# A packed 16-bit copy of the weights' high parts for the down projection's second matmul

## The chip, the cores and the metric

One core of one Trainium2 chip runs the whole kernel as one launch. The metric is the device time of that launch in microseconds; lower is better. A kernel is timed in several runs and its median is compared. Of each kernel one further execution is recorded by the hardware profiler; the profile's durations are from that one.

## What is computed

The reference is one layer of a hybrid decoder block on 512 tokens of width 2048, all in float32. The change lies in the last matrix product, the down projection of the gated feed-forward part:

```python
def conv_ffn(h, w_up, conv_w, conv_b, w_down):
    u = h @ w_up                                   # (512, 2048) @ (2048, 11264)
    ...                                            # three-tap convolution along the tokens
    val, gate = jnp.split(c, 2, axis=-1)
    return (jax.nn.silu(gate) * val) @ w_down      # (512, 5632) @ (5632, 2048)

def reference(x, ...):
    ...                                            # RWKV-7 mixing and windowed attention, gated
    x = x + (g_rw * p_rw + g_att * p_att) @ w_out[l]
    x = x + conv_ffn(rms_norm(x, norm2_g[l]), w_up[l], conv_w[l], conv_b[l], w_down[l])
    return x
```

## The kernel before

**Three matmuls for one product.** Every float32 product is made of three matmuls that add up in one PSUM tile. Each operand is split into a high part (ScalarE's copy to `float32r`, TensorE's reduced float32 format) and a low part (VectorE's difference of the operand and its high part, in bfloat16). The three are high x high, low x high and high x low. For the latter two the high part is taken as bfloat16, and there is no copy for that: `top(x)` views the float32r tile as 16-bit elements and takes every second one, the upper half of each word. So a tile of 1024 words is read as 1024 16-bit elements at a step of 4 bytes.

```python
    def top(x):
        x = x.bitcast(BF16)
        return x[(slice(None),) * (len(x.shape) - 1) + (slice(1, None, 2),)]
```

**The stages.** The program runs in this order: projections of the normed input (`project`, L284), among which attention and the recurrent mixing are woven; branch projections (L284 too, in `project`); the output projection; the up projection with the convolution; the down projection. In `project` the weights are the stationary operand and the activations the moving one. Its third matmul moves `top(xhi)`, or, once it exists, `x16`, a packed bfloat16 copy that lies in the second half of the tile `xlo` (the profile names it xlo). In the branch projections the activations are named `rhi, rlo, ahi, alo` and have no such copy.

**Output and down projection** are each cut into two by two blocks and made of seven block products in place of eight (`PRODUCTS`), on sums and differences of blocks. Each product accumulates in a set of four PSUM tiles, `X` or `Y` by turns, and is then added into the result (`taken_out`; for the down projection into `xa`, L1102, which the outputs are stored from). The sums of weight blocks were made long before by accumulating DMAs (`sums_along`, issued by SP and POOL) into DRAM. For the down projection the order of the work is: product i of seven, step c of 11 (`NB["dn"]`), half q of two.

**One step** is `steps_of` (L1070 on). The activations' part (`fetch`, L1064 on) is a 128 x 2 x 256 tile `hraw`, loaded by SP and split into `hhi` (ScalarE, L216) and `hlo` (VectorE, L217). For each q, SP loads a 128 x 1024 weight tile (L1078, six buffers), ScalarE makes `whi` (L1080), VectorE makes `wlo` (L1081), with three buffers of each. Here the roles are turned: the activations are stationary and the weights are the moving operand, 512 columns at a time. Twelve matmuls follow (L1090): three kinds by two row blocks by two column blocks. In the code's words the kinds are (stationary, moving) = (`hhi`, `whi`), (`hlo`, `top(whi)`), (`top(hhi)`, `wlo`); the profile writes a matmul's two inputs as moving,stationary: `whi,hhi` (float32), `whi,hlo` and `wlo,hhi` (16-bit). The order of the kinds alternates, `turns = ((0, 1, 2), (1, 2, 0))`: for q = 0 first whi,hhi, then whi,hlo, then wlo,hhi; for q = 1 first whi,hlo, then wlo,hhi, then whi,hhi. So whi,hhi matmuls of two tiles stand together.

**What sets the order around it.** Each engine takes its instructions in program order; waits between engines come from the tile framework, by who last wrote or read a buffer. So ScalarE's next `whi` waits for the last reader of the buffer three tiles back, and TensorE's matmuls wait for the splits. POOL (GpSimd) computes nothing in the output, up or down projection but two small memsets: it issues accumulating DMAs during the earlier stages, and at step 1 of the down projection's first product the four loads of `xa` (L1508). At that same point the pools of tiles of the up projection (`upcx`, `upx`) are closed and their memory becomes free.

Of the kernel before, what the change touches and what calls it, by code (L numbers as in the profile page):

```python
# [11 lines left out]
BF16 = mybir.dt.bfloat16  # L12
# [7 lines left out]
P = 128  # L20
# [115 lines left out]
def block_kernel(ctx: ExitStack, tc: tile.TileContext, d: Dims, a: dict, out: bass.AP):  # L136
    nc = tc.nc
    act, dve, pool, pe, sync = nc.scalar, nc.vector, nc.gpsimd, nc.tensor, nc.sync
# [54 lines left out]
    def rsqrt_small(pl, ss, scale, eps, mx=None, tag="rq"):  # L193
        n = ss.shape[-1]
        tl = [pl.tile([P, 8], F32, name=f"{tag}{i}", tag=f"{tag}{i}", bufs=2)[:, :n] for i in range(3)]
        v, y, t = tl
        if mx is not None:
            dve.tensor_scalar(v, ss, mx, None, op0=ALU.max)
        else:
            dve.tensor_scalar(v, ss, scale, eps, op0=ALU.mult, op1=ALU.add)  # L200
        dve.tensor_scalar(t.bitcast(I32), v.bitcast(I32), 1, None, op0=ALU.logical_shift_right)
        dve.tensor_scalar(y.bitcast(I32), t.bitcast(I32), -1, 0x5F3759DF, op0=ALU.mult, op1=ALU.add)
        dve.tensor_scalar(v, v, -0.5, None, op0=ALU.mult)
        for _ in range(3):
            dve.tensor_tensor(t, y, y, op=ALU.mult)
            dve.tensor_tensor(t, t, v, op=ALU.mult)
            dve.scalar_tensor_tensor(y, t, 1.5, y, op0=ALU.add, op1=ALU.mult)
        return y
# [11 lines left out]
    def quarter(w, src, c):  # L220
        return sum_d[w][src][c] if isinstance(src, str) else a["w_" + w][src[0], src[1], 2 * c : 2 * c + 2]

    jobs, up_jobs = [], []
    for f in range(NPRE):
        w, t = a["w_up"][f], {n: up_d[f, n] for n in ("s3", "s1", "P6", "P3")}
# [22 lines left out]
# [3 lines that stand above are left out]
# [45 lines left out]
    if True:  # L296
# [39 lines left out]
        def ztile(c0):  # L336
            acc = accp.tile([P, S], F32, name="acc", tag="acc")
            project(acc, zt[c0], xhi, xlo, x16 if scaled else None, first.pop(c0, ()))
            return acc
# [5 lines left out]
        r = rsqrt_small(p0, ssum, 1.0 / d.D, RMS_EPS)  # L345
# [58 lines left out]
        with ExitStack() as pt:  # L404
# [59 lines left out]
            for t in range(1, NKV):  # L464
                for c0, then in ((d.c_ka, keys), (d.c_va, values)):
                    acc = ztile(c0 + t * P)
# [25 lines left out]
            for g in range(NHK):  # L492
# [7 lines left out]
                for n in range(NT):  # L500
                    ts = slice(n * P, (n + 1) * P)
# [15 lines left out]
                    mx, es, den, rc = (st[:, i] for i in range(4))  # L517
# [34 lines left out]
        with ExitStack() as pr:  # L552
# [30 lines left out]
            acc = ztile(d.c_wd)  # L583
# [5 lines left out]
            acc = ztile(d.c_ad)  # L589
# [3 lines left out]
            for i in range(NG):  # L593
                acc = ztile(d.c_gd + i * P)
# [403 lines left out]
    hp0 = hps.enter_context(tc.tile_pool(name="hhlC", bufs=2, side="right", reuse_waits="tile"))  # L998
    wp["step"] = 12
    with ExitStack() as pbb:  # L1000
# [8 lines left out]
        for m, i in order:  # L1009
# [10 lines left out]
            acc = accp.tile([P, S], F32, name="acc", tag="acc")  # L1020
            project(acc, a["w_b"][m].rearrange("p (k c) -> p k c", c=P)[:, r0 : r0 + n], hi, lo)
            if second:
                w = min(XC, d.D)
# [31 lines left out]
    WC = KH * P  # L1055

    def raw_tile(nm="raw", n=6):
        return rwp.tile([P, WC], F32, name=nm, tag=nm, bufs=n)

    def banks(pl, nm):  # L1060
        return [[pl.tile([P, S], F32, name=f"{nm}{t}{q}") for q in range(NQW)] for t in range(NT // 2)]

    def fetch(w, i, c, pl, pin=free):

        hhi, hlo = (pl.tile([P, 2, TH], t, name=f"h{e}", tag=f"h{e}") for e, t in (("hi", F32R), ("lo", BF16)))
        hr = pl.tile([P, 2, TH], F32, name="hraw", tag="hraw")
        pin(sync.dma_start(hr, right_d[w][c][RIGHT_AT[PRODUCTS[i][3]]]))
        return lambda: split(hhi, hlo, hr, pin), hhi, hlo

    def steps_of(w, i, acc, c, pl, got=None):  # L1070

        _, start, src, _, _ = PRODUCTS[i]
        make, hhi, hlo = got or fetch(w, i, c, pl)
        if not got:
            make()
        for q in range(2):
            wr = raw_tile()
            sync.dma_start(wr, quarter(w, src, c)[q])  # L1078
            whi, wlo = (hlp.tile([P, WC], t, name=f"w{e}", tag=f"w{e}") for e, t in (("hi", F32R), ("lo", BF16)))
            act.activation(whi, wr, AF.Copy)  # L1080
            dve.tensor_tensor(wlo, wr, whi.bitcast(F32), op=ALU.subtract)  # L1081
            fst, lst = start and c + q == 0, c == NB[w] - 1 and q == 1
            order = turns[q]
            for j in order:
                for t in range(NT // 2):
                    ts = slice(t * P, (t + 1) * P)
                    for e in range(NQW):
                        dst, es = acc[t][e], slice(e * S, (e + 1) * S)
                        l, r = ((hhi[:, q, ts], whi[:, es]), (hlo[:, q, ts], top(whi[:, es])), (top(hhi[:, q, ts]), wlo[:, es]))[j]
                        pe.matmul(dst, l, r, start=fst and j == order[0], stop=lst and j == order[2],  # L1090
                                  skip_group_check=True)

    def taken_out(i, acc, xr, scale, done):
        ci, tj, sign = PRODUCTS[i][4]
        last = i in (3, 4, 5, 6)
        for t in range(NT // 2):
            for e in range(NQW):
                tt = tj * NT // 2 + t
                cs = slice(ci * DH + e * S, ci * DH + (e + 1) * S)
                x = xr(tt, cs)  # L1100
                if scale == 1.0:
                    dve.tensor_tensor(x, x, acc[t][e], op=ALU.add if sign > 0 else ALU.subtract)  # L1102
                else:
                    (pin if i == 6 else free)(
                        dve.scalar_tensor_tensor(x, acc[t][e], sign * scale, x, op0=ALU.mult, op1=ALU.add))
                if last:
                    done(i, tt, ci * NQW + e, cs)
# [264 lines left out]
    with tc.tile_pool(name="sqp", bufs=1, side="right", reuse_waits="tile") as sqp:  # L1372
        yx = ExitStack()
        py = yx.enter_context(tc.tile_pool(name="psY", bufs=1, space=PSUM, side="right", reuse_waits="tile"))
        acc = {"X": banks(px, "X"), "Y": banks(py, "Y")}
        for i in range(len(PRODUCTS)):
            nm = PRODUCTS[i][0]
# [98 lines left out]
    hp0 = upcx.enter_context(tc.tile_pool(name="hhl0", bufs=1, side="right", reuse_waits="tile"))  # L1476
# [3 lines left out]
    for i in range(4 * NPRE + 3, len(steps)):  # L1480
        run(i)
        if steps[i] == (NF - 2, "P7"):
            first_h = fetch("dn", 0, 0, hp0, pin)
# [8 lines left out]
    with ExitStack() as pd:  # L1492
        pxy = pd.enter_context(tc.tile_pool(name="psD", bufs=1, space=PSUM, reuse_waits="tile"))
        acc = {n: banks(pxy, n) for n in "YX"}
        for i in range(len(PRODUCTS)):
            nm = PRODUCTS[i][0]
            for c in range(NB["dn"]):
                if i == 0 and c == 1:
                    while later:
                        later.pop(0)()  # L1500
                    B[-1].keep()
                    upcx.close()
                    upx.close()
                    hp0 = pd.enter_context(tc.tile_pool(name="hhl", bufs=3, reuse_waits="tile"))
                    xp = pd.enter_context(tc.tile_pool(name="xacc", bufs=1, reuse_waits="tile"))
                    xa = xp.tile([P, NT, d.D], F32, name="xa")
                    for t in range(NT):
                        pool.dma_start(xa[:, t], x1_d[t * P : (t + 1) * P])  # L1508
                steps_of("dn", i, acc[nm], c, hp0, first_h if i == 0 and c == 0 else None)
            taken_out(i, acc[nm], lambda t, cs: xa[:, t, cs], 1.0, row_out)  # L1510


# [57 lines left out]
def build(nc, arrays, d):  # L1570
    aps = {
        k: nc.dram_tensor(f"in_{k}_dram", v.shape, mybir.dt.from_np(v.dtype), kind="ExternalInput").ap()
        for k, v in arrays.items()
    }
    out = nc.dram_tensor("out_0_dram", (S, d.D), F32, kind="ExternalOutput").ap()
    with tile.TileContext(nc) as tc:
        block_kernel(tc, d, aps, out)
# [11 lines left out]
```

## Time and profile before

| what | value |
| --- | --- |
| median of 3 runs | 2712.91 us (2708.49 to 2714.39) |
| the profiled execution | 2711.84 us, of which 2710.1 us span |
| TensorE matmul busy | 2670.9 us, 99% of the span |
| VectorE busy | 1961.6 us, 72% |
| ScalarE busy | 1332.1 us, 49% |
| POOL busy | 233.4 us, 9% |
| TensorE clock granted, mean | 0.997 |

PE is TensorE's matmuls, PEld its weight loads, DVE is VectorE, ACT ScalarE, POOL GpSimd, SP the engine that only issues DMAs. A row of a group reads: line, engine, operation, output<-inputs by tile name, shapes, x count, then busy us, mean ns of one, and after the bar the idle time of that engine just before such instructions and what ended it. A row of the chain or the timeline begins with the start and the length in us from the start of the span. Successive matmuls overlap in the records and their ends are modelled, so the mean of one is longer than its share of the time; the spacing of starts is the better measure of the rate.

### The profile page before, as it was taken

The page shows a single profiled execution, that of the slowest core. Times are in us where ns is not written, and L with a number is a line of the kernel's source. Part 1 is how long each engine was busy: PE and PEld are TensorE (multiplying, and loading weights), DVE is VectorE, ACT ScalarE, POOL GpSimd, SP SyncE. Part 2 cuts the span into 40 slices and gives each one's busy share as a digit, 9 for nine tenths or more (in the row PEclk, how much of TensorE's full clock was granted, in tenths as well). Part 3 has the DMA queues.
Part 4 walks back from the last instruction along what each step waited for, and adds up shares of the span by engine and source line. Part 5 has one row for each costly group of instructions (what it writes and reads, how often), then busy time and mean ns, then how long its engine had stood idle before and what let it go on. Part 6 is the DMA issues. An engine that isn't in the chain of part 4 may idle for free.

```text
span 2710.1 us, 45707 instructions
## 1 busy us (share of the span) xinstructions
PE 2670.9 (99%) x17410; PEld 1863.9 (69%) x17410; DVE 1961.6 (72%) x3380; ACT 1332.1 (49%) x2229; POOL 233.4 (9%) x322
## 2 busy tenths in 40 slices
PE   8999999999999999999999999999999999999999
PEld 4555566666666666555558898999999998555555
DVE  6787768776877774555678788888878888665655
ACT  6455445544544453322566555555554555444453
POOL 0001011111111101011000011111111110000000
PEclk9999999999999999999999999999999999999999
DMA  6566887889887778888776888988899888877775
GB/s 236 150 165 180 216 219 197 223 221 232 218 222 194 197 181 253 245 249 283 249 256 190 238 227 243 251 245 238 242 247 252 236 238 280 303 240 249 256 260 182
DMA packets 228331, 623.78 MB, mean 230 GB/s; under 512 B 24960, under 2 KB 45072, under 8 KB 227088
## 3 DMA queue, kind: packets, MB, share of 16 engines
q1 hardware_dynamic: 159552, 445.23, 49.8%
q0 software_dynamic: 37216, 136.33, 26.3%
q10 hardware_dynamic: 31344, 39.31, 4.2%
q8 instruction: 136, 2.23, 0.3%
q14 instruction: 83, 0.68, 0.1%
HBM read 571.16 MB, written 191.18 MB: 281 GB/s over the span
## 4 chain that ended last, share of the span: by engine, by line
PE 82%; DVE 8%; DMA 3%; issue 3%; ACT 2%; POOL 0%; SPq 0%; ACTq 0%; DVEq 0%; POOLq 0%
PE acc L284 26%; PE X L1227 16%; PE X L1090 11%; PE Y L1090 9%; PE Y L1227 8%; PE Z L1227 4%; DVE wlo L264 1%; PE psG L836 1%; PE psS L852 1%; PE bulk L711 1%; DMA raw<-in_w_z_dram 1%; PE bulk L760 1%; PE mi L541 1%; DVE wlo L1209 1%; PE psU L841 1%
## 5 line engine op out<-in xcount | busy, mean ns | idle before, releaser
L1081 DVE TENSOR_TENSOR wlo<-raw,whi 128x1024 bf16<-128x1024 f32 x210 | 256.7, 1225 | 192.7 <-ACT whi L1080 191.7
L284 PE MATMUL acc<-xhi,whi 128*128 128x512 f32 x1152 | 348.9, 427 | 10.9 <-ACT whi L263 10.4
L1080 ACT ACTIVATE whi<-raw 128x1024 fp32r<-128x1024 f32 x210 | 221.9, 1058 | 276.0 <-PE X L1090 119.5
L263 ACT ACTIVATE whi<-raw 128x512 fp32r<-128x512 f32 x352 | 218.8, 627 | 254.3 <-PE acc L284 151.4
L264 DVE TENSOR_TENSOR wlo<-raw,whi 128x512 bf16<-128x512 f32 x352 | 239.9, 688 | 136.8 <-ACT whi L263 113.9
L284 PE MATMUL acc<-xlo,whi 128*128 128x512 bf16 x1152 | 315.3, 382 | 0.5 <-ACT whi L263 0.3
L284 PE MATMUL acc<-xlo,wlo 128*128 128x512 bf16 x1072 | 292.9, 380 | 0.0
L1209 DVE TENSOR_TENSOR wlo<-raw,whi 128x1024 bf16<-128x1024 f32 x184 | 224.8, 1223 | 72.9 <-ACT whi L1207 72.1
L1227 PEld LDWEIGHTS <-wlo 128*128 128x128 bf16 x2464 | 237.1, 97 | 42.1 <-DVE wlo L1209 2.6
L284 PEld LDWEIGHTS acc<-xhi,whi 128*128 128x128 f32 x1152 | 212.6, 190 | 59.5 <-ACT whi L263 11.9
L1227 PEld LDWEIGHTS <-whi 128*128 128x128 bf16 x2464 | 228.3, 98 | 36.3 <-ACT whi L1207 2.3
L1207 ACT ACTIVATE whi<-a 128x1024 fp32r<-128x1024 f32 x124 | 130.7, 1054 | 229.8 <-DVE a L1202 210.9
L284 PEld LDWEIGHTS <-wlo 128*128 128x128 bf16 x1408 | 137.4, 99 | 149.6 <-issue 7.9
L284 PEld LDWEIGHTS <-whi 128*128 128x128 bf16 x1408 | 125.6, 100 | 151.0 <-issue 48.6
L1209 DVE TENSOR_TENSOR wlo<-a,whi 128x1024 bf16<-128x1024 f32 x124 | 151.9, 1225 | 64.0 <-ACT whi L1207 62.8
L1227 PE MATMUL X<-b,whi 128*128 128x256 f32 (+1 forms) x1472 | 195.7, 281 | 0.4 <-DVE u L1249 0.2
L1207 ACT ACTIVATE whi<-raw 128x1024 fp32r<-128x1024 f32 x184 | 192.1, 1046 | 5.7 <-PE Y L1227 2.6
L1227 PE MATMUL X<-t,whi 128*128 128x256 bf16 (+1 forms) x1408 | 186.2, 281 | 2.9 <-ACT u L1255 2.9
L1227 PE MATMUL Y<-t,whi 128*128 128x256 f32 (+1 forms) x1408 | 186.4, 280 | 0.3 <-DVE u L1257 0.3
L1090 PEld LDWEIGHTS <-hhi 128*128 128x128 bf16 x840 | 81.5, 97 | 103.9
L1090 PEld LDWEIGHTS <-hlo 128*128 128x128 bf16 x840 | 72.8, 97 | 107.4 <-issue 27.4
L1279 DVE SCALAR_TENSOR_TENSOR c<-u,par,c 128x512 f32<-128x512 f32 x176 | 131.4, 747 | 14.2 <-ACT c L1276 14.1
(390 smaller groups left out, 4593.9 us busy)
## 6 DMA issues: line engine op xcount, KB each, us to landing
raw<-in_w_up_dram SPq DMA_DIRECT2D x170, 512.0 KB
raw<-in_w_z_dram SPq DMA_DIRECT2D x288, 256.0 KB
s_dn<-in_w_dn_dram POOLq DMA_DIRECT2D x88, 512.0 KB, 7.2
raw<-s_dn SPq DMA_DIRECT2D x88, 512.0 KB
raw<-in_w_up_dram POOLq DMA_DIRECT2D x80, 512.0 KB, 8.2
raw<-in_w_dn_dram SPq DMA_DIRECT2D x66, 512.0 KB
s_dn<-in_w_dn_dram SPq DMA_DIRECT2D x44, 512.0 KB
s_dn<-s_dn SPq DMA_DIRECT2D x44, 512.0 KB
```

What stands on the lines that cost most here:

```text
L263: act.activation(hi, raw, AF.Copy)
L264: dve.tensor_tensor(lo, raw, hi.bitcast(F32), op=ALU.subtract)
L284: stream.append(pe.matmul(acc, l, r, start=k0 + j == 0, stop=k0 + n == nk and j == len(ops) - 1))
L541: pe.matmul(ps, vhl[:, n - 1 + kb, g].rearrange("p e c -> p (e c)"), phl[i][:, kb].rearrange("p h c -> p (h c)"), start=kb == kbs[0] and i ...
L711: pe.matmul(ps[:, j * 2 * P : (j + 1) * 2 * P], BKK[:, n0 + j], BAR[:, n0 + j].rearrange("p h a c -> p (h a c)"), start=True, stop=True)
L1080: act.activation(whi, wr, AF.Copy)
L1081: dve.tensor_tensor(wlo, wr, whi.bitcast(F32), op=ALU.subtract)
L1090: pe.matmul(dst, l, r, start=fst and j == order[0], stop=lst and j == order[2], skip_group_check=True)
L1207: pin(act.activation(hi, t, AF.Copy))
L1209: return lambda: pin(dve.tensor_tensor(lo, t, hi.bitcast(F32), op=ALU.subtract))
L1227: pin(pe.matmul(ps, l, r, start=start and k == 0 and i == way[0], stop=k == KH - 1 and i == way[2], skip_group_check=True))
L1279: pin(dve.scalar_tensor_tensor(t, u[:, i, j + 1 : j + 1 + S], cw[:, j + 1, ci : ci + 1], t, op0=ALU.mult, op1=ALU.add))
```

## The change

From the second of the seven products of the down projection on, a new pool `flat` with three buffers holds `w16`, a packed bfloat16 tile of 128 x 1024. For each weight tile POOL copies `top(whi)` into it, and the second kind of matmul moves `w16` in place of `top(whi)`. The numbers are the same, since the copy keeps the 16 bits. The first product of the down projection, and the whole output projection, which `steps_of` serves too, stay as they were, because `flat` is `None` there. The stationary operand `top(hhi)` of the third kind stays strided.

```diff
-    def steps_of(w, i, acc, c, pl, got=None):
+    def steps_of(w, i, acc, c, pl, got=None, flat=None):
...
             dve.tensor_tensor(wlo, wr, whi.bitcast(F32), op=ALU.subtract)
+            w16 = top(whi)
+            if flat:
+                w16 = flat.tile([P, WC], BF16, name="w16", tag="w16")
+                pool.tensor_copy(w16, top(whi))
             fst, lst = start and c + q == 0, c == NB[w] - 1 and q == 1
...
-                        l, r = ((hhi[:, q, ts], whi[:, es]), (hlo[:, q, ts], top(whi[:, es])), (top(hhi[:, q, ts]), wlo[:, es]))[j]
+                        l, r = ((hhi[:, q, ts], whi[:, es]), (hlo[:, q, ts], w16[:, es]), (top(hhi[:, q, ts]), wlo[:, es]))[j]
...
         acc = {n: banks(pxy, n) for n in "YX"}
+        flat = None
         for i in range(len(PRODUCTS)):
             nm = PRODUCTS[i][0]
+            if i == 1:
+                flat = pd.enter_context(tc.tile_pool(name="w16", bufs=3, reuse_waits="tile"))
...
-                steps_of("dn", i, acc[nm], c, hp0, first_h if i == 0 and c == 0 else None)
+                steps_of("dn", i, acc[nm], c, hp0, first_h if i == 0 and c == 0 else None, flat)
```

## The prediction, made before the changed kernel was run

> **What bounds the kernel now.** I read the page's shares first, then the chain of waits in order of time.
>
> ```profile
> PE 2670.9 (99%) x17410; PEld 1863.9 (69%) x17410; DVE 1961.6 (72%) x3380; ACT 1332.1 (49%) x2229; POOL 233.4 (9%) x322
> PE 82%; DVE 8%; DMA 3%; issue 3%; ACT 2%; POOL 0%; SPq 0%; ACTq 0%; DVEq 0%; POOLq 0%
> ```
>
> ```profile
> 2289.01 59.35 PE X L1090 x264
> 2348.36 59.33 PE Y L1090 x264
> ...
> 2585.67 59.33 PE Y L1090 x264
> 2644.99 58.64 PE X L1090 x261
> ```
>
> The second fence is the end of the chain: start, length, what. From 2289 us on the chain is nothing but the down projection's matmuls: seven block products of 264 matmuls, 59.33 us each, with nothing between. So here time is what TensorE's matmuls take, and only two things can change it: a shorter matmul, or a wait that opens a gap. Next, the same stretch by windows (PE, PEld, DVE, ACT, POOL busy, then the clock, DMA share, GB/s).
>
> ```profile
> 2289.01:2348.36 59.35, 59.35 (x265) 32.74 (x265) 40.36 (x47) 30.14 (x36) 2.15 (x4) 1.00 0.90 340
> 2348.36:2407.69 59.33, 59.33 (x265) 32.75 (x265) 35.97 (x39) 28.99 (x33) 0.00 (x0) 1.00 0.74 244
> 2585.67:2644.99 59.32, 59.32 (x265) 32.74 (x265) 35.91 (x39) 28.99 (x33) 0.00 (x0) 1.00 0.76 260
> ```
>
> PE has no gap and a granted clock of 1.00; DVE is busy 35.97 of 59.33 us; POOL does nothing from the second product on, which is where the change gives it work. Now the groups by line in five of those products (2348.36 to 2644.99 us), and the same view of an earlier stage, the branch projections (1060 to 1235 us); columns are busy us, then mean ns.
>
> ```profile
> L1081 DVE TENSOR_TENSOR wlo<-raw,whi 128x1024 bf16<-128x1024 f32 x110 | 134.8, 1225 | 114.2 <-ACT whi L1080 113.7
> L1080 ACT ACTIVATE whi<-raw 128x1024 fp32r<-128x1024 f32 x110 | 116.4, 1059 | 151.7 <-PE Y L1090 83.5 <-PE X L1090 55.7 <-DVE xa L1102 12.5
> L1090 PE MATMUL Y<-whi,hhi 128*128 128x512 f32 x264 | 73.0, 416 | 0.0
> L1090 PE MATMUL Y<-whi,hlo 128*128 128x512 bf16 x264 | 70.7, 389 | 0.0
> L1090 PE MATMUL Y<-wlo,hhi 128*128 128x512 bf16 x264 | 67.6, 378 | 0.0
> L217 DVE TENSOR_TENSOR hlo<-hraw,hhi 128x512 bf16<-128x512 f32 x55 | 37.6, 684 | 0.0
> L1102 DVE TENSOR_TENSOR xa<-xa,X 128x512 f32<-128x512 f32 x12 | 7.4, 682 | 1.6 <-PE X L1090 1.6
> ```
>
> ```profile
> L284 PE MATMUL acc<-ahi,wlo 128*128 128x512 bf16 x108 | 28.8, 387 | 0.0
> L284 PE MATMUL acc<-alo,whi 128*128 128x512 bf16 x109 | 28.2, 380 | 0.0
> L284 PE MATMUL acc<-xlo,wlo 128*128 128x512 bf16 x56 | 14.4, 379 | 0.0
> ```
>
> Both 16-bit products of L1090 stream 512 columns, yet the one with hlo takes 389 ns and the one with hhi 378. In the first the moving operand is the high halves of whi, every second 16-bit element; in the second it is the packed wlo, and the strided operand is the stationary one. The branch projections tell which of the two matters: there ahi,wlo has the strided operand moving and is slow (387), alo,whi has it stationary and is fast (380), and xlo,wlo, with both packed, is no faster (379). So the stride costs where it moves, and the change takes it from there.
>
> **The change part by part.** (a) What it makes shorter. In six products of 11 steps of 2 weight tiles there are 6 x 22 = 132 tiles, each with 4 matmuls of the hlo kind: 528 matmuls. By the groups' means each loses 389 - 378 = 11 ns: 528 x 11 = 5.8 us. Ends of matmuls are modelled, so I check against starts, on one pair of tiles in the timeline (start, length):
>
> ```profile
> 2403.05 1.08 PE L1090 MATMUL Y<-whi,hlo 128*128 128x512 bf16 x4
> 2403.97 1.02 PE L1090 MATMUL Y<-wlo,hhi 128*128 128x512 bf16 x4
> 2404.83 1.06 PE L1090 MATMUL Y<-whi,hlo 128*128 128x512 bf16 x4
> 2405.73 1.02 PE L1090 MATMUL Y<-wlo,hhi 128*128 128x512 bf16 x4
> ```
>
> Four hlo matmuls last 0.92 and 0.90 us, the four wlo ones between them 0.86: 0.10 us for the pair, and 66 pairs give 6.6 us. The 0.02 by which the first group is longer than the second sits behind the f32 matmuls; that is a handover, and the packed kind should pay some of it too: alo,whi, which stands behind f32 matmuls in the branch projections, has a mean 1 ns over xlo,wlo's 379. I take 5.8 us, and 5.3 (10 ns each, the two groups of 0.90 and 0.86 alone) to 6.6 as its bounds.
>
> By a rule of the Trainium skill (SBUF — State Buffer, § Door 1, the note on SBUF cachelines) consecutive reads in one 16-byte line run at full bandwidth, so a 16-bit operand at a step of 4 bytes, four reads to a line, should cost nothing, and this term would be 0. The rows above speak against it.
>
> (b) What it adds: 132 POOL copies, 128x1024 from every second to packed 16-bit elements. No POOL copy is in the trace, so I bound it by POOL's memsets, which write, and the ACT row above (1059 ns), which reads and writes as many elements in one pass:
>
> ```profile
> L612 POOL MEMSET BAR<- 64x1024 f32 x2 | 1.9, 952 | 0.1
> L613 POOL MEMSET BX<- 64x512 f32 x2 | 1.0, 520 | 0.1
> ```
>
> 1024 elements per partition take POOL 952 ns to write (0.84 ns an element and some 90 ns fixed). A copy is at least that, 0.95 us, and at most a read pass and a write pass in turn, 1.90 us. I take 1.06, the ACT row's, because that is the nearest instruction with the same in and out. A weight tile lasts 59.33 / 22 = 2.70 us on PE, so on its own even 1.90 us would be hidden: POOL would be busy 40 to 70%.
> The Trainium skill (GPSIMD Engine Reference, § 3.1) gives about 1.8 cycles an element at 1.2 GHz as the best of a tight loop, an estimate of 1.54 us here; no run here shows it, and the memsets show 1.0 cycle.
>
> (c) Who waits for it. The hlo matmuls now wait for w16 from POOL, not for whi, and behind a waiting matmul stands all of PE. The lead is long, as ACT runs three buffers ahead:
>
> ```profile
> 2402.33 1.06 ACT L1080 ACTIVATE whi<-raw 128x1024 fp32r<-128x1024 f32 x1 [2.50 <-PE Y L1090]
> 2403.42 1.23 DVE L1081 TENSOR_TENSOR wlo<-raw,whi 128x1024 bf16<-128x1024 f32 x1 [2.33 <-ACT whi L1080]
> 2408.45 1.08 PE L1090 MATMUL X<-whi,hlo 128*128 128x512 bf16 x4
> ```
>
> The tile that ACT finishes at 2403.39 takes the buffer of a tile whose last matmuls had just ended; it is third from there and its hlo matmuls start at 2408.45: 5.06 us of lead. A copy of 1.90 us that first waits out the 1.23 us of DVE's wlo is done after 3.13. So latency is covered, with 1.9 us to spare; throughput is what can fail (rival below). w16 has three buffers of its own. In even tiles whi is now let go after its f32 matmuls, 0.92 us earlier; ACT's next write also waits for the copy, which ends before those matmuls begin. Both cost nothing under that cover.
>
> (d) POOL's queue. Its last DMAs, the four loads of xa (2.15 us in the window row of the first product), are issued before the first copy, so no DMA is moved behind a copy. DVE, ACT and SP issue what they did. The new pool of tiles opens at the second product, in memory that the up projection has left a product earlier: at most one tile's wait, once, 0 to 2.7 us; I take 0, as a whole product of 59 us lies between.
>
> The sum: the profiled execution took 2711.84 us, 1.74 more than its span; less 5.8 gives 2706.0. The median of the runs shown, 2712.91, lies 1.07 higher, so against it I expect **2707.1**; with 5.3 to 6.6 and a run's scatter of some 2 us, 2704 to 2710 is this case's own range. 0.2% of the median, about what a measurement of this kernel tells from no change, is 5.4 us: the gain is just above it.
>
> **The rivals.**
> 1. DVE and POOL take turns. If a POOL copy that reads SBUF can't run while DVE's two-input operations do, their times add up. Per product DVE's busy 35.97 us leaves 23.36 us for 22 copies: 1.06 us each. This is the point that decides, and my copy of 1.06 stands exactly on it. At the middle of the bounds, 1.43 us, each tile is 0.37 us over: 132 x 0.37 = 49 us slower, 2762; at 1.90 it is 132 x 0.84 = 111 us, 2824. Once this pair sets the pace, the shorter matmuls bring nothing. For it: wlo and hlo read two SBUF operands and hold 27 + 7.5 us of a product, and a copy is released by the same ACT instruction as wlo, so the two always meet. Against it: no row of before has POOL reading beside DVE; xa (2.7 us a product) reads PSUM and one SBUF operand; a copy near the memset's 0.95 would fit even in turns.
> By the Trainium skill (SBUF — State Buffer, § Who interferes with whom) a DVE instruction with two SBUF inputs and a GpSimd instruction that reads SBUF block each other for the whole instruction; no run here shows it so far. Chance 0.32.
> 2. Nothing changes: the 11 ns are not the stride's, or stay (the hlo matmuls keep 0.90 us per four), or small waits eat them. 2711 to 2713 us. The branch rows speak against it. Chance 0.09.
> 3. The copy alone is slower than a tile, over 2.70 us. At 3.0 us it is 132 x 0.3 = 40 us, 2753. It would take three times the memset's time. Chance 0.04.
>
> **How the numbers follow.** The forecast, copies hidden and matmuls shorter, has 0.55: 0.40 of it ends over 5.4 us faster and 0.15 within, since 5.8 is so near the line and a copy just at the turning point would take some of it back. Rivals 1 and 3 are slower (0.36), rival 2 the same (0.09). So faster 0.40, same 0.24, slower 0.36. The range starts at 2703, under the forecast's own, and goes to 2762, rival 1's middle: what is left out is half of rival 1 and part of rival 3, under 0.2.
>
> **What would show it.** Right: hlo matmuls with w16 at 378 to 380 ns, four in 0.86 to 0.87 us; products two to seven at 58.4 us in the chain, the first still 59.35; POOL with 132 copies of about 1.06 us, DVE's wlo still 1225 ns, and no PE idle time released by POOL or DVE. Wrong: hlo at 387 ns (rival 2); wlo or the copies drawn out to 2 us or more, with PE idle before hlo or wlo matmuls and products over 59.33 us (rival 1); POOL busy nearly all the time with PE behind it (rival 3).

## The result and the profile after

The changed kernel takes 2706.99 us (median of 13 runs, 2700.71 to 2712.3) against 2712.91 us (13 runs, 2708.49 to 2716.03): ratio 0.9981, 95% interval 0.9973 to 0.9989. That is 5.9 us less, where 5.8 was forecast; by the interval it is 3.0 to 7.3 us less, so that the two agree to 0.1 us is chance. The profiled execution took 2708.84 us with a span of 2707.1; its down projection began 2.3 us later than before's, behind stages that the change doesn't touch, and that is scatter.

The end of the chain of waits of the changed kernel (start, length, what):

```profile
2291.28 59.35 PE X L1094 x264
2350.63 58.37 PE Y L1094 x264
...
2584.12 58.37 PE Y L1094 x264
2642.50 57.70 PE X L1094 x261
```

The first product is as long as it was; each later one is 0.96 us shorter, and TensorE still hands over to itself with nothing between. Six times 0.96 is 5.8 us: that is the whole difference, and firmer than the medians. The groups by line in five of those products (2350.63 to 2642.5 us; busy us, mean ns, idle before and its releaser):

```profile
L1085 POOL COPY w<-whi 128x1024 bf16<-128x1024 bf16 x110 | 187.5, 1731 | 104.5 <-ACT whi L1080 104.5
L1081 DVE TENSOR_TENSOR wlo<-raw,whi 128x1024 bf16<-128x1024 f32 x111 | 179.4, 1619 | 31.2 <-ACT whi L1080 31.1
L1094 PE MATMUL Y<-w,hlo 128*128 128x512 bf16 x264 | 68.1, 380 | 0.0
L1094 PE MATMUL Y<-wlo,hhi 128*128 128x512 bf16 x264 | 67.8, 379 | 0.0
L217 DVE TENSOR_TENSOR hlo<-hraw,hhi 128x512 bf16<-128x512 f32 x55 | 65.2, 1185 | 11.4 <-ACT hhi L216 11.4
```

The hlo matmuls (now w,hlo) went from 389 to 380 ns, as fast as the other 16-bit kind. But VectorE's wlo went from 1225 to 1619 ns and hlo from 684 to 1185, and a copy is recorded at 1731 ns. Two engines got much slower and the kernel got faster. The timeline of one pair of tiles shows how:

```profile
2399.57 1.22 DVE L1081 TENSOR_TENSOR wlo<-raw,whi 128x1024 bf16<-128x1024 f32 x1 [0.66 <-ACT whi L1080]
2401.04 1.20 DVE L217 TENSOR_TENSOR hlo<-hraw,hhi 128x512 bf16<-128x512 f32 x1 [0.24 <-ACT hhi L216]
2402.16 2.05 DVE L1081 TENSOR_TENSOR wlo<-raw,whi 128x1024 bf16<-128x1024 f32 x1
```

```profile
2399.60 2.10 POOL L1085 COPY w<-whi 128x1024 bf16<-128x1024 bf16 x1 [1.77 <-ACT whi L1080]
2401.64 1.50 POOL L1085 COPY w<-whi 128x1024 bf16<-128x1024 bf16 x1
```

The second fence is POOL in the same stretch: two copies back to back. The first wlo comes 0.03 us before the copy and is not slowed (1.22). Then hlo starts while the first copy runs and lasts 1.20 in place of 0.68; the second wlo starts while the second copy runs and lasts 2.05 in place of 1.22. One that comes second is late. The ends tell it best: the first copy ends 0.9 us after the first wlo, hlo 0.54 us after that copy, the second copy 0.9 us after hlo, the second wlo 1.07 us after that copy. This reads as turns, my rival 1, without its loss. The experiments had to say whether it is turns, and why they fit.

### The profile page after: what moved, and what is told of

Its sections match the earlier page's. It is cut to its first block, busy times and chain, and to the rows that moved or that the text cites. A ratio compares the mean times of both kernels' runs of the same rounds, so it can differ in the third digit from the quotient of the medians.

```text
span 2707.1 us, 46031 instructions
## 1 busy us (share of the span) xinstructions
PE 2664.5 (98%) x17410; PEld 1865.2 (69%) x17410; DVE 2045.0 (76%) x3380; ACT 1326.4 (49%) x2229; POOL 458.5 (17%) x454
## 4 chain that ended last, share of the span: by engine, by line
PE 83%; DVE 8%; DMA 4%; ACT 2%; issue 2%; SPq 0%; ACTq 0%; DVEq 0%
PE acc L284 26%; PE X L1231 16%; PE X L1094 11%; PE Y L1094 9%; PE Y L1231 8%; PE Z L1231 4%; PE psG L836 1%; DVE wlo L264 1%; PE psS L852 1%; PE bulk L711 1%; DMA raw<-in_w_z_dram 1%; DVE wlo L1213 1%; PE bulk L760 1%; PE mi L541 1%; DMA rsd<-rsT 1%
## 5 line engine op out<-in xcount | busy, mean ns | idle before, releaser
L1081 DVE TENSOR_TENSOR wlo<-raw,whi 128x1024 bf16<-128x1024 f32 x210 | 307.6, 1470 | 93.7 <-ACT whi L1080 93.1
L1080 ACT ACTIVATE whi<-raw 128x1024 fp32r<-128x1024 f32 x210 | 215.0, 1053 | 275.9 <-POOL w L1085 155.7
L1213 DVE TENSOR_TENSOR wlo<-raw,whi 128x1024 bf16<-128x1024 f32 x184 | 224.6, 1222 | 72.8 <-ACT whi L1211 72.1
L1085 POOL COPY w<-whi 128x1024 bf16<-128x1024 bf16 x132 | 225.5, 1734 | 176.3 <-ACT whi L1080 176.3
L1213 DVE TENSOR_TENSOR wlo<-a,whi 128x1024 bf16<-128x1024 f32 x124 | 151.9, 1225 | 64.0 <-ACT whi L1211 62.8
L1211 ACT ACTIVATE whi<-raw 128x1024 fp32r<-128x1024 f32 x184 | 192.3, 1047 | 6.6 <-PE Y L1231 2.6
L243 POOL DMA_DIRECT2D s_dn<-in_w_dn_dram x88 | 72.5, 824 | 695.4 <-DMA s_dn<-s_dn 290.8
L1199 POOL DMA_DIRECT2D raw<-in_w_up_dram x80 | 69.7, 871 | 547.3 <-DVE wlo L1213 260.9
```

The costliest lines, as they stand in the source:

```text
L243: return lambda: pool.dma_start(dst, second, accum_op=ALU.add, max_dma_last_dim=4096)
L1085: pool.tensor_copy(w16, top(whi))
L1199: pool.dma_start(w[n], a["w_up"][f, 1, int(n == "s1")], accum_op=ALU.add)
L1211: pin(act.activation(hi, t, AF.Copy))
L1213: return lambda: pin(dve.tensor_tensor(lo, t, hi.bitcast(F32), op=ALU.subtract))
```

## The experiments

Theory T: a copy takes 1.04 us by itself (the shortest in the records) and VectorE's two-input operations and the copy exclude each other; the gain comes from the moving operand alone. Rivals: the copy itself takes 1.7 us and only slows VectorE; the two don't hinder each other; the copies give or take time by other ways.

**Copies made, not used.**

```diff
-(hlo[:, q, ts], w16[:, es])
+(hlo[:, q, ts], top(whi[:, es]))
```

> POOL still makes every copy, but the matmuls go on moving the strided view of whi; the copies are read by nobody. Theory (turns: a copy of 1.04 us and VectorE's wlo and hlo exclude each other, and everything gained comes from the packed moving operand): no gain and no loss, 2712.9 us as before, products of 59.33 us in the chain, the hlo kind at 389 ns, copies still drawn out to 1.7 us and wlo to 1.6 us on average. Rival (the copies cost or give something by themselves, for example by when ScalarE may write the next whi): over 2 us away from 2712.9.

Measured: 2711.7 us, ratio 1.0 (0.9991 to 1.0009). The groups by line, 2360 to 2640 us:

```profile
L1085 POOL COPY w<-whi 128x1024 bf16<-128x1024 bf16 x104 | 179.6, 1752 | 100.8 <-ACT whi L1080 100.8
L1081 DVE TENSOR_TENSOR wlo<-raw,whi 128x1024 bf16<-128x1024 f32 x105 | 172.1, 1642 | 33.2 <-ACT whi L1080 33.1
L1094 PE MATMUL Y<-whi,hlo 128*128 128x512 bf16 x233 | 63.3, 389 | 0.5
```

Copies and wlo are drawn out as in the change, the strided matmuls are back at 389 ns, and the gain is gone. The copies cost nothing and give nothing.

**One copy, used by all.**

```diff
-                w16 = flat.tile([P, WC], BF16, name="w16", tag="w16")
-                pool.tensor_copy(w16, top(whi))
+                if "w16" not in wp:
+                    wp["w16"] = flat.tile([P, WC], BF16, name="w16", tag="w16")
+                    pool.tensor_copy(wp["w16"], top(whi))
+                w16 = wp["w16"]
```

> Only the first weight tile of the second product is copied, and that one packed tile is moved by all later matmuls of the hlo kind (so the low x high term of the down projection is wrong from there on: the copies are left out). Theory (turns, with room left): 2707.0 as with the copies, products of 58.37 us, wlo back at 1225 ns. Rival (the meeting of POOL and VectorE takes back a part of the gain): 1 us or more faster than the changed kernel, 2706 or less, with products under 58.3 us.

Measured: 2707.18 us, ratio 0.9979 (0.9970 to 0.9988), wlo at 1222 ns, hlo at 692, w,hlo at 380. With VectorE left alone nothing more is gained: the meeting of the two engines takes nothing back. The products last 58.37 us by the starts of their first matmuls, as in the changed kernel.

**No wlo for POOL to meet** (the operation on VectorE is made once and its tile moved by all later matmuls of that kind).

> VectorE's wlo is made for one tile of the second product only and moved by all later matmuls of that kind (the high x low term is left out of the down projection from there on). POOL copies every tile as in the change. Turns: copies meet only hlo, most of them 1.04 us, mean 1.05 to 1.2; products 58.37 us. Rival (the copy by itself takes 1.73 us and slows VectorE): mean stays 1.7 us.

Measured: 2705.42 us in its one run. The groups by line, 2360 to 2640 us:

```profile
L1091 POOL COPY w<-whi 128x1024 bf16<-128x1024 bf16 x106 | 107.3, 1040 | 173.9 <-ACT whi L1080 173.9
L217 DVE TENSOR_TENSOR hlo<-hraw,hhi 128x512 bf16<-128x512 f32 x53 | 59.5, 1123 | 208.6 <-ACT hhi L216 208.6
```

The copy is 1040 ns on average, so 1731 was not its own. And hlo, which here always comes after a copy has begun, bears all of the delay (1123 in place of 684) while the copy isn't slowed at all. A shared rate would slow both; this is one waiting for the other. VectorE's xa, which reads one operand in SBUF and one in PSUM, doesn't take turns: here it runs at its usual 0.68 us beside a copy of the usual 1.04.

```profile
2406.70 0.68 DVE L1112 TENSOR_TENSOR xa<-xa,Y 128x512 f32<-128x512 f32 x1
2406.76 1.04 POOL L1091 COPY w<-whi 128x1024 bf16<-128x1024 bf16 x1 [3.29 <-ACT whi L1080]
```

**More to copy, to find the point where it tips.** After each copy a second one into a tile `w17` that nobody reads, of all, half or a quarter of the columns:

```diff
                 pool.tensor_copy(w16, top(whi))
+                w17 = flat.tile([P, WC], BF16, name="w17", tag="w17", bufs=2)
+                pool.tensor_copy(w17[:, :K], top(whi[:, :K]))   # K = WC, WC // 2, WC // 4
```

> Each tile is copied twice, the second copy into a tile that nobody reads. Turns: the pair of tiles holds VectorE and POOL 4.64 us now; two more copies of about 1.0 us make it 6.6 to 6.7 against 5.31 of the matmuls, so 66 x 1.3 to 1.4 = 86 to 92 us slower than the changed kernel, about 2795, with PE idle before wlo or w matmuls. Rival (POOL works beside VectorE without hindering it, copies of 1.04 us): 4.2 us of POOL in 5.31, all hidden, 2707. Rival (the copy by itself takes 1.73 us): POOL alone needs 3.46 us a tile against 2.65, 107 us slower, about 2814, with POOL busy all the time.

> After each copy POOL copies half of the tile once more (512 elements per partition) into a tile that nobody reads. Turns: a half copy is 0.5 to 0.55 us, the pair of tiles holds VectorE and POOL 4.64 + 1.0 to 1.1 = 5.7 us against 5.31, 66 x 0.4 = 26 us slower than the changed kernel, about 2733. Rival (the copy by itself takes 1.73 us, VectorE is only slowed): 1.73 + 0.87 = 2.60 us a tile against 2.65, still hidden, 2707. Rival (no hindrance): 2707.

> The same with a quarter (256 elements). Turns: a quarter copy is about 0.3 us, 4.64 + 0.6 = 5.24 us of 5.31: just hidden, 2707 to 2710. This and the half copy enclose the point where the turns begin to set the pace, by my reckoning at 0.33 us more a tile. The other theories: 2707.

Measured: twice 2776.18 us (one run); and a half 2718.83, ratio 1.0020 (1.0011 to 1.0030); and a quarter 2707.16, ratio 0.9977 (0.9967 to 0.9988). Without a wait the second copy takes 1033, 607 and 393 ns. Busy time by windows from 2415 to 2640 us (PE, PEld, DVE, ACT, POOL), first of the kernel with a quarter more, then with a half more, then with twice the copy:

```profile
2415.00:2640.00 225.00, 225.00 (x1020) 126.75 (x1019) 167.49 (x141) 106.58 (x127) 220.68 (x171) 1.00 0.82 258
```

```profile
2415.00:2640.00 225.00, 217.26 (x975) 121.37 (x974) 192.57 (x136) 103.00 (x122) 225.00 (x164) 1.00 0.80 249
```

```profile
2415.00:2640.00 225.00, 191.49 (x830) 105.05 (x844) 167.67 (x124) 93.02 (x107) 225.00 (x142) 1.00 0.69 215
```

With the quarter PE has no idle time; with the half it has 8 us, with twice 34, and these waits are for POOL:

```profile
PE Y L1096 <- POOL w L1085: 20.8, 22, 1.9
PE X L1096 <- POOL w L1085: 20.1, 20, 1.9
```

(the kernel with twice the copy, 2360 to 2640 us: total us, times, longest). The kernel without hindrance, 2707 for all three, is out. So is the copy of 1.73 us, by which the half would have been hidden. The direction is that of turns, but the sizes were not: the half was to cost 26 us and cost 11.8, twice was to cost 86 to 92 and cost 69.2. The timeline of the kernel with a half more shows why (POOL, then VectorE):

```profile
2502.80 1.04 POOL L1085 COPY w<-whi 128x1024 bf16<-128x1024 bf16 x1
2503.78 1.60 POOL L1087 COPY w<-whi 128x512 bf16<-128x512 bf16 x1
2505.33 1.50 POOL L1085 COPY w<-whi 128x1024 bf16<-128x1024 bf16 x1
2506.77 1.60 POOL L1087 COPY w<-whi 128x512 bf16<-128x512 bf16 x1
```

```profile
2503.01 1.89 DVE L1081 TENSOR_TENSOR wlo<-raw,whi 128x1024 bf16<-128x1024 f32 x1 [0.64 <-ACT whi L1080]
2504.83 1.09 DVE L217 TENSOR_TENSOR hlo<-hraw,hhi 128x512 bf16<-128x512 f32 x1
2505.85 2.05 DVE L1081 TENSOR_TENSOR wlo<-raw,whi 128x1024 bf16<-128x1024 f32 x1
```

Put in order of their ends (start plus length), the operations of the two engines follow each other without a break, and always by the same steps: wlo ends 1.07 us after the operation before it, hlo 0.54, a copy 0.90, a half copy 0.47, and a copy 0.98 behind one of POOL's own. So an operation holds its turn for some 0.14 us less than its recorded length by itself (1.22, 0.68, 1.04, 0.61). A pair of tiles of this kernel adds up to 5.52 us, of the kernel with twice the copy to 6.37, and their steady products last about 11 times that, some 60.8 and 70.1 us. Over 66 pairs this is 14 and 70 us more than the changed kernel, beside 11.8 and 69.2 measured; the first of the six products loses less, since it starts with the lead of the engines.

By the same steps the change needs 2 x 1.07 + 0.54 + 2 x 0.90 = 4.49 us of the 5.31 that the matmuls of a pair take. That leaves 0.82 us a pair, 0.41 a copy: an estimate from these steps is that it tips at a copy of about 1.45 us. A quarter more is 0.60 us a pair and fits; a half more is 1.03 and doesn't. My forecasts were too high because they started from 4.64 us, in which the first wlo, which nothing precedes in the change, stands with its whole length, and because they counted a further whole copy as 1.0 us where it adds 0.94.

**The copy on ScalarE.**

```diff
-                pool.tensor_copy(w16, top(whi))
+                act.activation(w16, top(whi), AF.Copy)
```

> ScalarE makes the packed copy in place of POOL. The matmuls gain the same 5.8 us; ScalarE gets 22 x 1.05 = 23 us more a product, 28.7 + 23 = 52 of 58.37 us, and VectorE is left alone (wlo 1225 ns). Theory: 2707, as the changed kernel, if ScalarE's queue still runs ahead; its next whi then stands behind a copy, and with 6 us of room a product a wait may show: 2707 to 2712. Rival (the gain needs POOL, or ScalarE becomes the bound): over 2713.

Measured: 2706.58 us, ratio 0.9974 (0.9962 to 0.9985); ScalarE's copy takes 1040 ns, wlo is at 1225, products 58.37 us. The gain doesn't need POOL; an engine with room for 1.04 us in 2.65 is enough.

**Packed operands in the up projection too.** Its third kind of matmul moves the strided high parts of seven factors that are made once and used by 44 column blocks, so seven copies would serve 2464 matmuls.

```diff
+        pin(act.activation(halves(bq[n][2]), top(halves(bq[n][0])), AF.Copy))
...
-(wlo[:, k], top(xh[:, k]))
+(wlo[:, k], x16[:, k])
```

> On top of the change: the up projection's third kind moves a packed 16-bit copy of each of its seven factors' high parts (made once each by ScalarE, 7 x 2048 elements per partition) in place of every second element. Theory (a strided moving operand costs by its columns): 11 ns for 512 columns is 5.5 for 256, less by the starts of the records, 113.6 against 109 ns, so 2464 matmuls x 4.5 to 5.5 ns = 11 to 14 us less than the changed kernel, minus up to 7 x 1.9 us of ScalarE if nothing hides it: 2693 to 2700. Rival (256 columns hide the cost of the stride, the spacing has another cause): 2707 or more.

Measured: 2714.19 us, ratio 1.0000 (0.9991 to 1.0009): a miss, 7 us slower than the changed kernel. The start of the stage lost 6.7 us beside the changed kernel (its first 1000 matmuls, 136.4 against 129.7 us), where ScalarE makes the copies; that these cause the loss is likely, but no run tests it apart. The steady part gained nothing, though the matmuls of the third kind did become shorter: from 1800 to 2200 us they start 109.3 ns apart in place of 113.6. To see why, the same kernel and the changed one once more, both with a part of VectorE's work left out:

> As the kernel with packed factors in the up projection, and besides VectorE's last tap of the convolution is left out (two of four VectorE operations of 747 ns a block; the third tap is missing from the result). If in the steady part of the up projection a loop through VectorE and ScalarE takes back what the packed operand gives, freeing VectorE by 1.5 us of 19.2 a block gives it free: 1000 matmuls there in 112.7 us in place of 114.2, about 9 us under its control. Rival (the spacing of matmuls has another cause, or ScalarE alone is the bound): the same 114.2 us, no difference to the control beyond the 6.6 us that the start of the stage lost.

> The control to the run before: the changed kernel, without the packed factors, and with the same tap left out. TensorE is the bound in the up projection of the changed kernel, so less VectorE work brings nothing: 114.2 us for 1000 matmuls, 2705 to 2707 us. If VectorE were the bound there: 10 us or more faster.

```diff
-                pin(dve.scalar_tensor_tensor(t, u[:, i, j + 1 : j + 1 + S], cw[:, j + 1, ci : ci + 1], t,
-                                             op0=ALU.mult, op1=ALU.add))
+                if j == 0:
+                    pin(dve.scalar_tensor_tensor(t, u[:, i, 1 : 1 + S], cw[:, 1, ci : ci + 1], t,
+                                                 op0=ALU.mult, op1=ALU.add))
```

Measured: 2699.46 us (ratio 0.9952, 0.9939 to 0.9966) and 2700.06 (0.9957, 0.9941 to 0.9972). The windows from 1800 to 2200 us of four kernels, in this order: the changed one, with packed factors, the control, with packed factors and less VectorE work. Count the matmuls, the first x:

```profile
1800.00:2200.00 400.00, 400.00 (x3504) 364.40 (x3502) 328.07 (x398) 212.17 (x293) 44.88 (x52) 1.00 0.89 241
```

```profile
1800.00:2200.00 400.00, 397.65 (x3504) 365.41 (x3502) 326.86 (x395) 212.50 (x294) 44.91 (x52) 1.00 0.89 242
```

```profile
1800.00:2200.00 400.00, 400.00 (x3506) 364.64 (x3505) 305.26 (x356) 215.04 (x292) 44.84 (x52) 1.00 0.89 245
```

```profile
1800.00:2200.00 400.00, 400.00 (x3549) 370.97 (x3547) 308.38 (x361) 218.22 (x297) 44.87 (x52) 1.00 0.89 245
```

Shorter matmuls alone: 3504, as without. Less VectorE work alone: 3506. Both: 3549, 1.3% more. In the steady up projection TensorE's stream and the loop through VectorE and ScalarE are so evenly matched that relieving one shows the other. (VectorE is busy 82% of that window, so it is the loop, with its waits, and not VectorE's busy time alone.) In the chain of the kernel with packed factors TensorE's share there is broken by ACT, DVE and issue, where it was TensorE alone before:

```profile
1828.03 5.71 PE X L1232 x48
...
1844.57 1.64 PE Z L1232 x16
1846.21 0.27 ACT u L1260
1846.48 0.71 ACT c L1281
1847.19 0.96 ACT whi L1212
1848.21 1.10 issue
1849.31 0.41 DVE u L1264
```

The control's total missed its expectation (2705 to 2707): its steady part is as forecast, but its first 2000 matmuls take 238.9 us in place of 245.2, so that VectorE does help to set the pace at the start of the stage. With packed factors and less VectorE work those 2000 take 245.2 us and the next 5000 563.8 in place of 570.7: what is lost at the start, the steady part earns back, and the two totals are alike. So the 9 us that the run with packed factors was to be under its control came out as 0.6; its steady part is as forecast (112.8 us for 1000 matmuls against 114.2).

**Packed operands in more stages with the same code**: the first product of the down projection from its second step on (`flat` opened at that point, copies by POOL), and the output projection (ScalarE, two buffers).

> The packed copy also for the first product of the down projection from its second step on (20 tiles, by POOL) and for all of the output projection (56 tiles, by ScalarE, two buffers). Each tile is worth 4 x 11 = 44 ns. If ScalarE's copies are hidden in the output projection as they are in the down projection: 76 x 0.044 = 3.3 us under the changed kernel, about 2703.5, products of the output projection 21.25 us in place of 21.6 and the first of the down projection 58.4 in place of 59.35. Rival (in the output projection ScalarE stands behind the ends of products with its squares and stores, and the copy makes the next whi late): 2707 or more, with PE idle after ACT there.

Measured: 2712.64 us, ratio 1.0003 (0.9994 to 1.0012), about 5.6 us slower than the changed kernel. Products two to six of the output projection did become 21.23 us, as forecast, but TensorE waits 1.5 us in all for ScalarE's copies in its first and last product, and the stage up to the up projection takes 155.5 us, as in the changed kernel. The larger loss is in the first product of the down projection, which took 66.3 us in place of 59.35. Waits of PE from 2289 to 2356 us, and its timeline:

```profile
PE X L1094 <- POOL w L1085: 4.7, 1, 4.7
```

```profile
2302.11 1.03 PE L1094 MATMUL X<-wlo,hhi 128*128 128x512 bf16 x4
2307.86 1.86 PE L1094 MATMUL X<-w,hlo 128*128 128x512 bf16 x4 [4.72 <-POOL w L1085]
2309.52 1.91 PE L1094 MATMUL X<-wlo,hhi 128*128 128x512 bf16 x4
```

There VectorE and ScalarE still finish the up projection's convolution, ScalarE's whi comes late (after 6.9 us of waiting, by the profile for VectorE's tq, a part of the convolution), the copy after it, and TensorE waits 4.7 us. Which of these began the delay no run separates. After the wait four matmuls last 1.86 and 1.91 us in place of 1.03 (the granted clock is 0.95 over this product, 1.00 in the next). No kernel here that computes the whole result beat the changed one beyond its interval; the two that leave out a tap of the convolution did, by some 7 us.

## Why the prediction was right

- **The term (a)**, 528 matmuls by 11 ns, held: 5.8 us, product by product. The packed matmuls run at 380 ns, in groups of 1.03 to 1.04 us, as the branch projections' rows had told. With copies that nobody reads the gain is gone, and with one copy for all it is the same. That it is the stride and not something about whi alone shows in the other tiles: ahi in the branch projections (387 ns) and the factors of the up projection (113.6 ns from start to start at 256 columns, 109.3 packed). The Trainium skill's note on cachelines (SBUF — State Buffer, § Door 1) would have made this term 0; the runs disagree, at 389 against 380 ns.
- **The price of a copy (b)**, 1.06 us taken from ScalarE's row, measured 1.04. That another engine's row came so near was in part luck: no row of POOL had shown a copy, and the middle of my bounds was 1.43. The upper bound of 1.90 was far off: a copy takes hardly longer than the 0.95 of a memset, which only writes. The estimate of 1.54 us from the Trainium skill's 1.8 cycles an element (GPSIMD Engine Reference, § 3.1) was too slow as well: from 512 to 1024 elements the copy grows by 1040 - 607 = 433 ns, 0.85 ns an element.
- **The lead (c)** and **POOL's queue (d)** held: PE never waits for POOL in the changed kernel. A copy, with its wait for VectorE, mostly ends 2.8 to 3.1 us before the first matmul that moves it.
- **Rival 1** had the right mechanism and the wrong room. VectorE and POOL do take turns, and it is as the Trainium skill says (SBUF — State Buffer, § Who interferes with whom): of a copy and a VectorE operation with two SBUF inputs, the second waits for the first, here by 0.4 to 1.1 us. I had taken 1.06 us of room for each copy by subtracting VectorE's whole busy time, which put the copy of 1.04 at the edge; with the shorter products of 58.37 us the same reckoning leaves 1.02, so by it the copies would just have set the pace. The forecast had the copies hidden because POOL would work beside VectorE; they are hidden because the turns fit, and that part of it is luck. The runs show more room because an operation holds its turn for less than its record: the five operations of a pair of tiles are 2 x 1.225 + 0.685 + 2 x 1.04 = 5.2 us by their lengths, and 4.49 us by their turns, against 5.31. About 0.14 us of each operation overlaps with its neighbour, and xa, which I had subtracted too, doesn't take turns. A copy has about as much that doesn't grow with its size: 607 - 433 = 0.17 us.
- **The signs to look for** were wrong in one point: I had written that wlo at 1225 ns would confirm the forecast and that wlo drawn out to 2 us would mean rival 1 and slower products. It was drawn out to 2.05 us in every second tile, and the products were shorter all the same, because the turns of a pair fit into its 5.31 us and ScalarE's whi is mostly done 4.9 us or more before the first matmul that moves its copy.

## What to carry to other kernels

A 16-bit moving operand read at every second element cost TensorE about 5% of its streaming time here, so a packed copy pays where TensorE alone sets the pace and some engine has a free microsecond a tile; it did not pay in the first product of the down projection, where ScalarE and VectorE were still behind. A slower record on another engine is no loss as long as its work, with all its turns, fits in the step and runs ahead; the way to know the margin is to add work until it tips. Where PE is busy all the time and a loop through other engines is just behind it, as in the up projection here, a shorter matmul gives nothing until that loop is relieved too.

## What the runs showed of the hardware

POOL's copy of 128x1024 16-bit elements from every second element takes 1.04 us, 0.85 ns an element and some 0.17 us besides, the same as ScalarE's 1040 ns. POOL's record of an instruction includes the time that it stands behind VectorE: the same copy is recorded at 1.04 to 2.13 us. A copy that waited ends 0.90 us after the VectorE operation it waited for. The 5.8 us of the change come from 512 columns in about 218 ns in place of 228 by the spacing of starts within the groups of hlo matmuls.
